# Norms of the first 400 tokens from squared columns, in an encoder layer on one core

## The chip, the core and the metric

The kernel runs on one core of one Trainium2 chip. The core has five engines with a queue of their own each: TensorE (PE; its weight loads are listed apart as PEld), VectorE (DVE), ScalarE (ACT), GpSimd (POOL) and SyncE (SP), which here issues nearly all transfers. A queue works strictly in its order; an instruction that waits holds up what stands behind it. The metric is the device time of one execution in microseconds (us), lower is better.

## What is computed

One layer of a hybrid encoder, run on a prompt of 256 tokens and a sample of 2048 tokens, each with 16 learned meta tokens ahead. Everything is float32.

```python
def rmsnorm(x, w):
    xf = x.astype(jnp.float32)
    y = xf * lax.rsqrt(jnp.mean(xf * xf, axis=-1, keepdims=True) + NORM_EPS)
    return (y * w.astype(jnp.float32)).astype(x.dtype)

def hybrid_layer(z, norm_w, w_in, q_norm_w, k_norm_w, sink, conv_w, conv_b, ln_w, ln_b, w_out):
    h = rmsnorm(z, norm_w)
    proj = jnp.einsum('bld,de->ble', h, w_in)
    q, k, v, g_att, c_val, c_glu, g_conv = jnp.split(proj, SPLIT_IDX, axis=-1)
...
    att = windowed_gqa(q, k, v, sink).reshape(B, L, W_ATT) * jax.nn.silu(g_att)
    cnv = conformer_conv(c_val, c_glu, conv_w, conv_b, ln_w, ln_b) * jax.nn.silu(g_conv)
    mixed = jnp.concatenate([att, cnv], axis=-1)
    return z + jnp.einsum('ble,ed->bld', mixed, w_out)
```

The change concerns the first line alone, `rmsnorm`, and of it the first 400 tokens (16 meta tokens and three blocks of 128).

## The kernel before

The tokens are kept as columns: `zt` is the transposed input, 1024 model dimensions as 8 slices of 128 partitions, and the 2320 columns are cut into six groups, the first of 400 columns (group 0), the others of 384. For each group a `Prep` object makes the normalised columns in two parts: `xh`, the value rounded to the form that TensorE multiplies in one pass, and `xl`, the rest. The weights of a unit of 256 output columns are split in the same way into `ws` high and low. One product of a group with half a unit is then 24 matmuls in one PSUM bank (8 slices by three passes: high by `xh`, high by `xl`, low by `xh`), and `pj` is the tile that it writes. The loop `items` runs over units and groups: the first two units take group 0, 1 and 2 in turn, so that the first four `pj` tiles, 96 matmuls, belong to group 0 and the next four to group 1. Then follow the other units, the convolution on DVE, attention and the output product.

How a group is prepared: `stats(i)` loads the rows of block i (`xn`, tokens on partitions; block 0 is the meta tokens), squares them on ACT with a running sum (`ssq`), and two POOL instructions (line 122 multiplies and adds, line 123 raises to the power -0.5) leave the factor in column i of `rstd`. `Prep.first` turns the factors of a group into a row `bc` in PSUM, the same on all partitions, by products with the identity. `Prep.scale(q)` multiplies two slices of `xt`, the loaded columns, by the norm weight and `bc` on DVE (line 681). `Prep.split(q)` rounds them on ACT into `xh` (line 698) and takes the differences `xl` (line 707), of each pair of slices the even one on DVE, the odd one on POOL. `weights(k)` loads a unit's weights as four pieces `wraw`, rounds each on ACT (line 742) and takes the low part on DVE or POOL (line 743).

What sets the order: a scheduler of the language places each engine's instructions by a time that it works out itself, except where a stretch is marked as `manual_schedule` for some engines or an instruction is pinned with `keep_in_program_order`; those keep the order in which the code is written. Transfers go out on SP in the order of its queue, over eight rotating semaphores, so that an issue waits until the transfer eight places earlier has landed. A tile is allocated from a pool with a fixed number of buffers, and a load into a buffer waits until its last reader is done: `xt` has four buffers, `us` (also used for `xn` of blocks 0 to 5 and for the second unit's `wraw`) four, `xn` of the later blocks two.

## Time and profile before

| | us |
|---|---|
| median of 3 runs (lowest, highest) | 976.84 (975.87, 977.05) |
| the profiled execution | 974.79 |
| its span, from the first to the last instruction | 973.0 |
| PE busy in the span | 949.2 |
| DVE, ACT, POOL busy | 755.9, 424.6, 341.2 |

The profile gives, for one execution, the start and length of every instruction, in us from the start of the span, and for an idle stretch the instruction or transfer that ended it. A row of the timeline merges equal instructions that follow each other: start, length from the first start to the last end, engine, line, operation, tile written and read, shape, count, and in brackets the idle time before it with what ended it. An ACT instruction that also sums its output shows as two rows. A float32 product with the identity is two matmuls in the profile.

### The profile page before, as it was taken

To read this page: it belongs to the slowest core of one execution; us is meant where nothing else is said; L and a number is where in the kernel's file an instruction comes from. 1 tells how busy PE (TensorE), PEld (TensorE's weight loads), DVE (VectorE), ACT (ScalarE), POOL (GpSimd) and SP (SyncE) were. 2 spreads that over 40 slices of the span, in tenths; PEclk is the share of its full clock that TensorE was granted. 3 is DMA by queue.
4 is the path that set the end of the run, shared out by engine and by line. 5 is a ranking of instruction groups with operands and counts; after the bars stand their busy time and mean duration, and the time that the engine had idled before them with its cause. 6 is when DMAs were issued, how large, how long until landed. Compare 5 with 4: busy or idle time off the path is not lost.

```text
span 973.0 us, 16234 instructions
## 1 busy us (share of the span) xinstructions
PE 949.2 (98%) x5740; PEld 890.0 (91%) x5740; DVE 755.9 (78%) x1261; ACT 424.6 (44%) x1156; POOL 341.2 (35%) x541
## 2 busy tenths in 40 slices
PE   5999999999999999999999998899999999999998
PEld 5999999999999999999999998678888888888886
DVE  4759999998987699999993555877776777767772
ACT  6621111343468710111113454766665666666651
POOL 5500000364468300000002464745445544544451
PEclk9999999999999999999999998999999999999999
DMA  9643345785735222233335657954554445544321
GB/s 332 221 181 118 130 170 179 264 286 182 225 124 180 92 73 76 86 128 136 127 135 173 212 141 219 294 171 134 159 177 148 125 152 166 178 127 135 109 88 43
DMA packets 113872, 155.75 MB, mean 160 GB/s; under 512 B 10592, under 2 KB 77296, under 8 KB 113792
## 3 DMA queue, kind: packets, MB, share of 16 engines
q1 hardware_dynamic: 113648, 154.11, 48.1%
q0 software_dynamic: 144, 0.62, 0.4%
q8 instruction: 45, 0.74, 0.3%
q14 instruction: 35, 0.29, 0.1%
HBM read 101.00 MB, written 54.31 MB: 160 GB/s over the span
## 4 chain that ended last, share of the span: by engine, by line
PE 91%; DMA 3%; DVE 2%; POOL 1%; issue 1%; SPq 1%; ACT 0%; POOLq 0%; DVEq 0%
PE pj L767 42%; PE y L538 20%; PE pj L783 13%; PE O L464 5%; PE pT L429 4%; PE S L316 4%; DMA woraw<-in_w_out 2%; DMA snk<-in_sink 1%; DMA wraw<-in_w_in 1%; PE O L316 1%; PE lnt L183 1%; PE qT L316 1%; PE lnu L202 1%; PE kt L941 0%; PE pT_m L426 0%
## 5 line engine op out<-in xcount | busy, mean ns | idle before, releaser
L767 PE MATMUL pj<-xh,ws 128*128 128x384 f32 (+1 forms) x1536 | 397.2, 339 | 2.5 <-ACT xh L698 2.5
L850 DVE SCALAR_TENSOR_TENSOR y<-us,cw,y 128x1167 f32<-128x1167 f32 x240 | 329.0, 1428 | 0.6
L767 PEld LDWEIGHTS pj<-xh,ws 128*128 128x128 f32 x1536 | 282.3, 189 | 2.8 <-ACT xh L698 2.8
L767 PE MATMUL pj<-xl,ws 128*128 128x384 f32 (+1 forms) x768 | 262.5, 342 | 0.1
L783 PE MATMUL pj<-ws,xh 128*128 128x256 f32 (+1 forms) x880 | 165.8, 286 | 0.0
L767 PEld LDWEIGHTS pj<-xl,ws 128*128 128x128 f32 x768 | 144.7, 188 | 1.1 <-POOL xl L707 0.7
L783 PEld LDWEIGHTS pj<-ws,xh 128*128 128x128 f32 (+1 forms) x880 | 137.8, 189 | 0.3
L783 PE MATMUL pj<-ws,xl 128*128 128x256 f32 (+1 forms) x440 | 125.4, 285 | 0.0
L383 ACT ACTIVATE sb<-sb,nm 128x304 f32<-128x304 f32 (+4 forms) x144 | 77.1, 535 | 45.3 <-DVE nm L371 43.7
L538 PE MATMUL y<-wo,mch 128*128 128x512 f32 x288 | 95.9, 414 | 0.0
L538 PE MATMUL y<-wo,mah 128*128 128x512 f32 x288 | 93.7, 406 | 0.0
L441 DVE TENSOR_TENSOR pl<-pT,ph 128x512 fp32r<-128x512 f32 x100 | 69.0, 690 | 29.0 <-ACT ph L440 28.5
L875 ACT ACTIVATE go<-pj 128x384 f32<-128x384 f32 x48 | 23.6, 491 | 154.5 <-PE pj L767 145.3
L371 DVE CUSTOM_DVE_ANT_0 sb<-S,bias,nsnk 128x304 f32<-128x304 f32 (+4 forms) x144 | 73.5, 511 | 15.0 <-PE S L316 14.5
L783 PEld LDWEIGHTS pj<-ws,xl 128*128 128x128 f32 (+1 forms) x440 | 83.2, 189 | 0.2
L122 POOL TENSOR_SCALAR ssk<-ssk 128x2 f32<-128x2 f32 x18 | 6.4, 356 | 213.0 <-ACT sqk L889 212.9
L440 ACT CAST ph<-pT 128x512 fp32r<-128x512 f32 x100 | 58.2, 583 | 40.2 <-PE pT L429 39.5
L406 POOL TENSOR_SCALAR sb<-sb,es 128x304 f32<-128x304 f32 (+4 forms) x144 | 72.8, 525 | 3.6
L316 PEld LDWEIGHTS S<-kw,q 128*128 128x128 f32 x288 | 53.8, 191 | 17.9 <-DVE nm L371 5.9
L122 POOL TENSOR_SCALAR ssq<-ssq 128x4 f32<-128x4 f32 (+2 forms) x55 | 28.3, 515 | 114.4 <-ACT xn L632 76.9
L316 PE MATMUL S<-kw,q 128*128 128x304 f32 (+4 forms) x288 | 62.6, 299 | 5.3 <-DVE nm L371 5.3
L429 PE MATMUL pT<-ident,sb 128*128 128x128 f32 x400 | 61.6, 274 | 1.3 <-POOL sb L406 1.0
(118 smaller groups left out, 1441.8 us busy)
## 6 DMA issues: line engine op xcount, KB each, us to landing
wd<-ws SPq DMA_DIRECT2D x36, 512.0 KB, 5.7
ws<-wd SPq DMA_DIRECT2D x36, 512.0 KB, 5.3
wraw<-in_w_in SPq DMA_DIRECT2D x52, 256.0 KB, 5.6
xn<-in_z SPq DMA_DIRECT2D x18, 512.0 KB, 5.7
gd<-go SPq DMA_DIRECT2D x48, 192.0 KB, 2.1
yo<-in_z SPq DMA_DIRECT2D x36, 256.0 KB, 2.6
out_y<-yo SPq DMA_DIRECT2D x36, 256.0 KB, 2.4
kw<-kd SPq DMA_DIRECT2D x16, 512.0 KB, 5.7
```

Of the source, the lines that this page charges most:

```text
L316: r = f(*a, **k)
L371: nc.vector.tensor_tensor_reduce(out=sb[:, n, c0:c1], in0=ps[:, 0:w], in1=cst["bias"][:, kv, n, c0 - QB * n : c1 - QB * n], scale=1.0, sca ...
L383: nc.scalar.activation(sb[:, n, c0:c1], sb[:, n, c0:c1], AF.Exp, bias=nm[:, n : n + 1], scale=-1.0, accum_out=rs[:, n : n + 1],)
L406: nc.gpsimd.tensor_scalar(sb[:, k, a0:a1], sb[:, k, a0:a1], es[:, k : k + 1], 1.0, op0=ALU.mult, op1=ALU.mult)
L429: nc.tensor.transpose(pt[:, hl, :], sbt[b, kv][:, hl, KCOL[k] : KCOL[k] + P], ident)
L440: nc.scalar.copy(ph, pt)
L441: nc.vector.tensor_tensor(pl, pt, ph, op=ALU.subtract)
L464: nc.tensor.matmul(o, lhs, t, start=(start and i == 0), stop=(stop and i == 1))
L538: nc.tensor.matmul(ps, mh[mi][:, e % 4, :], wo[e, wi][:, cols], start=(e == 4 and k == 0), stop=(e == 3 and k == 2),)
L767: nc.tensor.matmul(ps[:, :n], ws[:, d, wi, P * half_i : P * half_i + P], x[xi][:, d, o : o + n], start=(k == 0), stop=(k == 3 * ND - 1),)
L783: nc.tensor.matmul(ps[:rows, :UW], x[xi][:, d, o : o + rows], ws[:, d, wi, :], start=(k == 0), stop=(k == 3 * ND - 1),)
L850: nc.vector.scalar_tensor_tensor(y[:, yo + o0 : yo + o1], u[:, o0 + k : o1 + k], cw[:, j, k : k + 1], y[:, yo + o0 : yo + o1], op0=ALU.mul ...
```

## The change

The rows of blocks 0 to 3 are no longer loaded. The columns of group 0 are the first transfers. ACT squares each of the eight slices of 128x400 (`Prep.sums`), DVE adds them up in one tile, and four products with a column of ones (`ssq0`) sum over the partitions. DVE multiplies and adds, two POOL instructions raise to the power, and `first` goes on as before. TensorE multiplies the identity by itself into an unused tile `heat` 18 times ahead of these products, 8 times behind them and 6 times behind `first`. ACT, DVE and POOL keep the written order in this stretch (`MAN0`), and a few later instructions are pinned.

```diff
+MAN0 = {mybir.EngineType.Activation, mybir.EngineType.DVE, mybir.EngineType.Pool}
...
+    ones = const.tile([P, 1], F32, name="ones")
+    nc.vector.memset(ones, 1.0)
...
-                nc.scalar.activation(xn[:rows], xn[:rows], AF.Square, accum_out=ssq[:rows])
+                square = nc.scalar.activation(xn[:rows], xn[:rows], AF.Square, accum_out=ssq[:rows])
+                if i < 7:
+                    tc.keep_in_program_order(square)
...
+        def busy(pt, n):
+
+            for _ in range(n):
+                tc.keep_in_program_order(nc.tensor.matmul(pt[:, :P], ident, ident, start=True, stop=True))
...
+            def segments(self):
+                segs = [(0, NM, 0)] if self.g == 0 else []
+                return segs + [(blk_local(b)[1], P, b + 1) for b in range(3 * self.g, 3 * self.g + 3)]
+
+            def sums(self):
+
+                n = self.n
+                acc = None
+                for q in range(4):
+                    sq = cp.tile([P, UWID], F32, tag="us", name=f"sq{q}")[:, : 2 * 400].rearrange("p (d n) -> p d n", n=400)
+                    for dd in range(2):
+                        nc.scalar.activation(sq[:, dd, :n], self.xt[q][:, dd, :n], AF.Square)
+                        if acc is None:
+                            acc = sq[:, 0, :n]
+                        else:
+                            nc.vector.tensor_tensor(acc, acc, sq[:, dd, :n], op=ALU.add)
+                ps = psum.tile([P, 512], F32, tag="c", name="ssq0")
+                for o, rows, i in self.segments():
+                    tc.keep_in_program_order(
+                        nc.tensor.matmul(ps[:rows, i : i + 1], acc[:, o : o + rows], ones, start=True, stop=True)
+                    )
+                for rows, c0, c1 in ((P, 1, 4), (NM, 0, 1)):
+                    dst = rstd[:rows, c0:c1]
+                    nc.vector.tensor_scalar(dst, ps[:rows, c0:c1], 1.0 / D, EPS, op0=ALU.mult, op1=ALU.add)
+                    nc.gpsimd.tensor_tensor(dst, dst, half[:rows, 0 : c1 - c0], op=ALU.pow)
+
             def first(self):
...
-                    nc.tensor.matmul(
+                for o, rows, i in self.segments():
+                    pin(g == 1 and i == 4)(nc.tensor.matmul)(
...
-                nc.scalar.copy(hi, raw[q])
+                cast = nc.scalar.copy(hi, raw[q])
+                if k == 1:
+                    tc.keep_in_program_order(cast)
...
-        r = {i: stats(i) for i in (0, 1, 2, 3)}
+        for q in range(4):
+            preps[0].load(q)
         nc.sync.dma_start(vec, vecs)
-        preps[0].load(0)
-        preps[0].load(1)
         w01[0][0](nc.sync)
-        preps[0].load(2)
-        preps[0].load(3)
         nc.sync.dma_start(cw, conv_w)
         nc.vector.scalar_tensor_tensor(kscale, vec[:, 20:21], -(HD ** -0.5), vec[:, 21:22], op0=ALU.mult, op1=ALU.mult)
-        for i in (0, 1, 2, 3):
-            r[i]()
-        preps[0].first()
-        preps[0].alloc()
-        preps[0].scale(0)
-        for q in range(4):
-            if q < 3:
-                preps[0].scale(q + 1)
-            preps[0].split(q)
-            w01[0][1](q, nc.gpsimd if q % 2 else nc.vector)
+        heat = psum.tile([P, 512], F32, tag="d", name="heat")
+        with tc.manual_schedule(engines=MAN0):
+            busy(heat, 18)
+            preps[0].sums()
+            busy(heat, 8)
+            for q in range(4):
+                w01[0][1](q, nc.vector if q < 2 else nc.gpsimd)
+            preps[0].first()
+            busy(heat, 6)
+            preps[0].alloc()
+            preps[0].scale(0)
+            for q in range(4):
+                if q < 3:
+                    preps[0].scale(q + 1)
+                preps[0].split(q)
```

The change moves instructions beyond its own lines, since the scheduler lays out the rest anew. Three places matter below. The first is the start of DVE's queue from the last additions of the squares to the first difference `xl`; `sq_150` is the tile of the sum, `ws_0` the first unit's weights. Before:

```order
L998 SCALAR_TENSOR_TENSOR kscale<-vec 128x1
L681 SCALAR_TENSOR_TENSOR xt_0_116<-xt_0_116,vec,bc_151 128x400 x2
L681 SCALAR_TENSOR_TENSOR xt_1_118<-xt_1_118,vec,bc_151 128x400 x2
L743 TENSOR_TENSOR ws_0_120<-wraw_0_121,ws_0_120 128x2x256
L707 TENSOR_TENSOR xl_157<-xt_0_116,xh_156 128x400
```

Now:

```order
L1030 SCALAR_TENSOR_TENSOR kscale<-vec 128x1
L679 TENSOR_TENSOR sq_150<-sq_150,sq_159 128x400
L679 TENSOR_TENSOR sq_150<-sq_150,sq_164 128x400 x2
L687 TENSOR_SCALAR rstd<-ssq_169 128x3
L687 TENSOR_SCALAR rstd<-ssq_169 16x1
L778 TENSOR_TENSOR ws_0_118<-wraw_0_119,ws_0_118 128x2x256
L778 TENSOR_TENSOR ws_0_118<-wraw_1_121,ws_0_118 128x2x256
L714 SCALAR_TENSOR_TENSOR xt_0_109<-xt_0_109,vec,bc_194 128x400 x2
L714 SCALAR_TENSOR_TENSOR xt_1_111<-xt_1_111,vec,bc_194 128x400 x2
L740 TENSOR_TENSOR xl_206<-xt_0_109,xh_205 128x400
```

Additions, two small instructions and two weight differences now stand ahead of the first scaling, and the three last additions stand behind `kscale`, which needs the transfer `vec`.

The second place is PE's queue around the factors of group 1 (`bc_317` before, `bc_359` now); `pj_290` and `pj_353` before, `pj_332` and `pj_395` now, are the third and fourth tile of group 0. Before:

```order
L767 MATMUL pj_260<-xl_157,ws_0_120 128x400
L767 MATMUL pj_260<-xh_156,ws_0_120 128x400
L661 MATMUL bc_317<-ident,rstd 128x128 x2
L767 MATMUL pj_290<-xh_156,ws_1_196 128x400
L767 MATMUL pj_290<-xl_157,ws_1_196 128x400
L661 MATMUL bc_317<-ident,rstd 128x128
```

Now, at the end of the third tile and at the first matmuls of group 1:

```order
L802 MATMUL pj_332<-xh_205,ws_1_238 128x400 x2
L802 MATMUL pj_332<-xl_206,ws_1_238 128x400
L802 MATMUL pj_332<-xh_205,ws_1_238 128x400
L319 MATMUL bc_359<-ident,rstd 128x128 x3
L802 MATMUL pj_395<-xh_205,ws_1_238 128x400 x2
```

```order
L802 MATMUL pj_395<-xh_205,ws_1_238 128x400
L319 MATMUL bc_470<-ident,rstd 128x128 x3
L802 MATMUL pj_443<-xh_363,ws_0_118 128x384
L802 MATMUL pj_500<-xh_363,ws_0_118 128x384
L802 MATMUL pj_526<-xh_363,ws_1_238 128x384
L802 MATMUL pj_443<-xl_364,ws_0_118 128x384
```

The factors of group 1 came after 48 matmuls of group 0 and now come after 80 of its 96 (all 24 of `pj_332` and 8 of `pj_395` in between), those of group 2 (`bc_470`) now stand ahead of group 1's first matmul.

The third place is ACT's queue over the same stretch; `xn_389` to `xn_393` are the rows of blocks 7 to 9, which group 2 needs, `sg_1_0` is the sigmoid of `pj_332`. Before:

```order
L810 ACTIVATE sg_0_0_258<-pj_233 128x400
L698 CAST xh_321<-xt_0_213 128x384 x2
L698 CAST xh_321<-xt_1_217 128x384 x2
L698 CAST xh_321<-xt_2_221 128x384
L632 ACTIVATE xn_347,ssq_389<-xn_347 128x1024
```

Now:

```order
L845 ACTIVATE sg_0_0_300<-pj_275 128x400
L635 ACTIVATE xn_389,ssq_431<-xn_389 128x1024
L635 ACTIVATE xn_391,ssq_435<-xn_391 128x1024
L635 ACTIVATE xn_393,ssq_439<-xn_393 128x1024
L845 ACTIVATE sg_1_0_357<-pj_332 128x400
L731 CAST xh_363<-xt_0_255 128x384 x2
```

The squares of three blocks now stand ahead of the first rounding of group 1, which they stood behind or among.

More of the change, by code (lines that the diff above doesn't have):

```diff
@@ L656, in first @@
                 bc = psum.tile([P, 512], F32, tag="c", name=f"bc{g}")
-                segs = [(0, NM, 0)] if g == 0 else []
-                for b in range(3 * g, 3 * g + 3):
-                    segs.append((blk_local(b)[1], P, b + 1))
-                for o, rows, i in segs:
-                    nc.tensor.matmul(
+                for o, rows, i in self.segments():
+                    pin(g == 1 and i == 4)(nc.tensor.matmul)(
                         bc[:, o : o + rows],
```

## The prediction, made before the changed kernel ran

> **What bounds the kernel now.** I read the page first, then the chain of waits, then the timeline of the first 50 us.
>
> ```profile
> span 973.0 us, 16234 instructions
> PE 949.2 (98%) x5740; PEld 890.0 (91%) x5740; DVE 755.9 (78%) x1261; ACT 424.6 (44%) x1156; POOL 341.2 (35%) x541
> 16.46 8.36 PE pj L767 x40
> 24.82 0.44 PE bc L661 x4
> 25.85 12.23 PE pj L767 x68
> 39.28 20.75 PE pj L767 x118
> ```
>
> PE is busy for 949.2 of 973.0 us, and from 16.46 on the chain (start, length, what) stays on PE at least to 60 us. 68 matmuls of mostly 400 columns in 12.23 us are 0.18 each, 118 of 384 columns in 20.75 are 0.176, and a product with the identity is two matmuls of 0.11, 0.22 together. So only the time by which PE gets through groups 0 and 1 counts; what it gains or loses there goes to the end undiminished. Its start:
>
> ```profile
> 13.00 1.04 PE L767 MATMUL pj<-xh,ws 128*128 128x400 f32 x2 [2.46 <-ACT xh L698]
> 24.66 0.61 PE L661 MATMUL bc<-ident,rstd 128*128 128x128 f32 x4
> 10.57 2.25 DVE L681 SCALAR_TENSOR_TENSOR xt<-xt,vec,bc 128x400 f32<-128x400 f32 x4 [2.54 <-PE bc L661]
> 11.90 0.62 ACT L742 CAST ws<-wraw 128x512 fp32r<-128x512 f32 x1 [3.12 <-DMA wraw<-in_w_in]
> 13.00:18.20 5.20, 5.07 (x13) 4.04 (x14) 1.00 1.05 400
> 18.20:24.66 6.46, 6.46 (x36) 6.28 (x35) 1.00 1.05 379
> ```
>
> The first `pj` matmul starts at 13.00: scaling began at 10.57, but ACT waited until 11.90 for the weights. The first 48 matmuls (two tiles) are through at 24.66, where `bc` of group 1 begins; of these, 13 start in the first 5.2 us and the rest at 0.18 each (windows: length, PE busy, weight loads, granted clock). So 24.66 is the mark that the change has to beat.
>
> **The change part by part: the factors.** Four transfers of `xt` (400 KB each) take the place of 64 KB and three times 512 KB, the same 1600 KB.
>
> ```profile
> 7.63 1.06 ACT L632 ACTIVATE xn<-xn 128x1024 f32<-128x1024 f32 x1 [0.18 <-DMA xn<-in_z]
> 7.87 0.16 DVE L998 SCALAR_TENSOR_TENSOR kscale<-vec 128x1 f32<-128x1 f32 x1 [7.00 <-DMA vec<-in_vecs]
> 13.37 0.94 ACT L698 CAST xh<-xt 128x400 fp32r<-128x400 f32 x2
> 13.35 0.57 DVE L707 TENSOR_TENSOR xl<-xt,xh 128x400 fp32r<-128x400 f32 x1
> 9.14 0.54 POOL L123 TENSOR_TENSOR rstd<-ssq,half 128x1 f32<-128x1 f32 x1
> 12.75 0.69 DVE L743 TENSOR_TENSOR ws<-wraw,ws 128x512 fp32r<-128x512 f32 x1
> ```
>
> The last bytes are in at 7.6, `vec` lets `kscale` end at 8.0. The last two squares cost what two roundings of this shape cost, 0.94, and end at 8.6. But three additions stand behind `kscale`, each needs the one before, and each costs what a difference of this shape does, 0.57, with 0.07 between: 8.0 + 3 x 0.64 = 9.9. Four products with the column of ones are eight matmuls that load full weights, at 0.11: 10.8. DVE's small instruction is put at `kscale`'s 0.16: 11.1. Then two powers of 0.54 one behind the other: 12.2. So much if nothing disturbs POOL. But DVE's next rows are two weight differences of 0.69, and POOL and DVE get in each other's way:
>
> ```profile
> 13.54 1.52 POOL L743 TENSOR_TENSOR ws<-wraw,ws 128x512 fp32r<-128x512 f32 x1 [3.86 <-ACT ws L742]
> 14.35 1.14 DVE L707 TENSOR_TENSOR xl<-xt,xh 128x400 fp32r<-128x400 f32 x1 [0.44 <-ACT xh L698]
> 32.48 2.33 DVE L707 TENSOR_TENSOR xl<-xt,xh 128x384 fp32r<-128x384 f32 x3
> 34.48 0.74 POOL L123 TENSOR_TENSOR rstd<-ssq,half 128x1 f32<-128x1 f32 x1
> 29.02 2.08 POOL L707 TENSOR_TENSOR xl<-xt,xh 128x384 fp32r<-128x384 f32 x2 [1.28 <-ACT xh L698]
> ```
>
> A difference on DVE of 0.57 that starts at 14.35, while POOL works until 15.06, ends at 15.49: 0.43 behind POOL. A power at 34.48, beside the last of three DVE differences (to 34.81), takes 0.74, not 0.54. Taking turns, power, difference, power, difference, the second power ends at 13.3. The products of `first` begin with the meta block, whose factor is that second power. They take 4 x 0.22, so scaling starts at about 14.4 (13.3 without collisions: the 8 identity products, 1.8 from 10.8, end at 12.6, then 0.9 less what overlaps). Before, it started at 10.57.
>
> The Trainium skill, page "SBUF — State Buffer", section "Who interferes with whom", says that a DVE instruction with two SBUF inputs and a GpSimd instruction that reads SBUF exclude each other for the whole instruction, whoever comes first. By it the collisions are certain and the start is 14.4, not 13.3; the 1.14 above agrees.
>
> **From scaling to PE at work.** The weights no longer decide, having come earlier. DVE does four scalings (2.25) before the first `xl`. ACT rounds slice 1 by 1.7 after the start of scaling (0.62, 0.94, waits of 0.07), and POOL then takes its difference, 1.04 (half of 2.08). DVE's first `xl` comes 0.43 behind it: 1.7 + 1.04 + 0.43 = 3.2 (2.8 if DVE is first). Until then PE has but two matmuls to do, behind 6 identity products (1.3). So it resumes at 14.4 + 3.2 = 17.6 and does the other 46 in 46 x 0.18 = 8.3: 25.9 against 24.66, **1.2 later** (-0.1 with 13.3 and 2.8; the end above is the clock's, below).
>
> **Group 1.** The second edit is not in the diff: `bc` of group 1 now stands behind 80 matmuls, not 48.
>
> ```profile
> 39.32 4.29 DVE L681 SCALAR_TENSOR_TENSOR xt<-xt,vec,bc 128x384 f32<-128x384 f32 x8 [3.87 <-PE bc L661]
> 43.52 2.88 DVE L707 TENSOR_TENSOR xl<-xt,xh 128x384 fp32r<-128x384 f32 x3
> 32.06 0.42 SPq L626 DMA_DIRECT2D xn<-in_z  x1
> 36.56 1.06 ACT L632 ACTIVATE xn<-xn 128x1024 f32<-128x1024 f32 x1 [2.33 <-POOL xl L707]
> ```
>
> Behind it DVE needs eight scalings, 4.2, and its first `xl`, 1.1 behind POOL (the first 1.1 of the 2.88): 5.3. PE has 16 matmuls (2.9), three products of `bc` for group 2 (0.7) and three matmuls with `xh` (0.5): 4.1. It then waits 1.2. ACT is no earlier: its squares of blocks 7 to 9 now stand ahead of the sigmoid and of the first `xh`, and block 9's row is loaded into a buffer that block 7's square has to free. From that issue to the next square went 4.5 in the row at 32.06, with one more transfer ahead; that puts the first roundings about where DVE ends its scalings and POOL's differences a turn later. I take **1.5** (0.5 if the turns fall well, 2.5 if block 9 takes the full 4.5). Before, this cover was 48 matmuls, and no wait of PE is listed there. The number of all other products is the same; from group 2 on there is a tile's time to spare on each side.
>
> **The clock.** The 32 identity products lie beside the wait for factors and are hidden, save in the 12.6 above. Their use depends on this:
>
> ```profile
> 1.01 0.29 POOL masks.py:199 TENSOR_SCALAR_AFFINE_SELECT ident<-ident 128x128 f32<-128x128 f32 x1
> 599.44 0.73 PE L316 MATMUL S<-kw,q 128*128 128x176 f32 x2 [3.42 <-DVE nm L371]
> 595.10:598.50 3.40, 0.92 (x9) 0.71 (x6) 0.20 (x1) 0.84 (x2) 0.00 (x0) 1.00 0.91 283
> 598.50:605.30 6.80, 5.86 (x27) 5.86 (x28) 5.98 (x19) 5.10 (x15) 4.29 (x7) 0.50 0.74 240
> 622.40:625.80 3.40, 1.78 (x6) 0.78 (x6) 3.30 (x7) 2.74 (x9) 2.76 (x6) 1.00 1.07 374
> 623.34 1.57 PE L429 MATMUL pT<-ident,sb 128*128 128x128 f32 x4 [1.04 <-POOL sb L406]
> 625.80:629.20 3.40, 3.07 (x11) 2.69 (x11) 3.36 (x7) 1.86 (x5) 2.22 (x3) 0.50 1.09 352
> ```
>
> The granted clock falls to 0.50 for 3.4 or 6.8 us after 3.4 us in which PE was busy 0.92, or 1.78. In the new start PE can multiply the identity from 1.4 on. If the slow pace lasts as long as the 5.2 us at 13.00, it does twelve of the 18 at 0.44 and six at 0.22, done at 7.9. It is idle to 9.9, 2.0 us, and again from about 16 to 17.6. Either gap can leave an interval of 3.4 us half idle, and 3.4 us at half pace cost 1.7: in full behind 17.6, and 1.0 ahead of it, where 0.7 (12.6 to 13.3) lie beside the powers. Nothing is lost if both gaps fall across two intervals. I take **0.8**, between none and the 2.7 of both, since 1.78 busy was too little.
>
> The Trainium skill, page "TensorE: Matmul & The Clock Gate", section "Why this matters for your kernels", warns only of gaps above about 3 us. By it these gaps cost nothing and the sum is 2.7. The rows disagree: the longest wait in the interval from 622.40 was 1.04, and the clock fell.
>
> **Sum.** 1.2 + 1.5 + 0.8 = 3.5 later. The profiled execution took 974.79 (span 973.0, 1.8 around it), so 978.3 of its kind; the median of the runs, 976.84, is 2.05 above it, so 980.3 of theirs.
>
> **Rivals.** *Faster: a warm PE with early factors.* The half-pace stretch from 13.0 to 18.2 costs before (5.2 - 13 x 0.18 = 2.9), and the change removes it if scaling starts early enough. Were `vec` in 0.5 sooner, the products with ones one pass (0.5), the powers undisturbed and `first` at 0.11 each, scaling would start at 11.6; 2.8 later is 14.4, plus 8.3 gives 22.7, 2.0 sooner, and with no wait at group 1 the time is 974.8. For it: ACT's wait for weights is gone. Against: `kscale` and the power rows. It decides from a start of scaling at 11.7 down. *No change: turns fall well.* Scaling at 13.3, `xl` 2.8 behind, clock kept: -0.1, and 1.0 at group 1, 977.7. For it: POOL's first `xl` and DVE's start only 0.5 apart. Against: two powers and two differences are bound to meet. *The clock isn't held at all.* The identity products are then work for nothing: four, eight and four products at twice 0.22 add 3.5 less the 0.7 beside the powers, and a slow pace of 5.2 us behind 17.6 adds 2.6; with the 2.7 that is 8.1, 984.9. For it the row at 622.40; against it, PE works six us without a break at first. *The loss is absorbed later* at the waits near 600 us: no row before 590 us shows PE idle, so these start as much later; 976.8, hardly.
>
> **How the numbers follow.** A change counts as faster or slower beyond 0.2%, 2.0 us, about what a measurement of this kernel can tell. Forecast, 2 to 6.4 later (1.2 + 2.5 + 2.7 at most): 0.65. Clock not held at all: 0.05. No change by well-placed turns 0.17, by absorption 0.03. Faster, 0.1. So slower 0.7, same 0.2, faster 0.1. The range reaches from 976.0, just below the well-placed turns with no wait at group 1, to 983.2, the forecast with the clock lost twice; left out are the faster case and the clock never held, under 2 in 10. The forecast's own range is 978.8 to 983.2.
>
> **What would show it.** The first scaling (line 714) at 14.4, behind powers (line 688) that take over 0.6 or start over 0.6 apart; the second `pj` pair's last matmul near 26; a wait of PE for DVE's `xl` of 1 to 2 us near 37, and `bc` of group 2 ahead of it; for the clock, products at half pace for some 3 us between 10 and 21, or none. A start of scaling before 12, or group 1 without a wait, would make the prediction wrong.

## The result, and the profile after

The changed kernel took 980.37 us (median of 8 runs, 978.31 to 982.49), the kernel before 976.85 beside it (8 runs, 975.87 to 978.76): a ratio of 1.0035 with a 95% interval of 1.0022 to 1.0047, 3.5 us slower. The forecast was 980.3. The profiled execution took 979.06, that of the kernel before 974.79, which is 2.1 below its median; so the ends of two single executions are not compared below.

The head of the page of the changed kernel, then TensorE's timeline (start, length, instruction, count, idle time ahead of it and what ended that):

```profile
span 977.3 us, 16381 instructions
PE 957.2 (98%) x5812; PEld 899.5 (92%) x5812; DVE 756.0 (77%) x1271; ACT 423.5 (43%) x1156; POOL 337.6 (35%) x535
```

```profile
1.35 6.80 PE L647 MATMUL heat<-ident 128*128 128x128 f32 x36 [1.35 <-POOL ident masks.py:199]
10.05 0.96 PE L683 MATMUL ssq<-ones,sq 128*16 128x1 f32 x8 [1.90 <-DVE sq L679]
10.87 2.03 PE L647 MATMUL heat<-ident 128*128 128x128 f32 x16
13.78 1.25 PE L319 MATMUL bc<-ident,rstd 16*128 16x16 f32 x8 [0.87 <-POOL rstd L688]
14.87 1.50 PE L647 MATMUL heat<-ident 128*128 128x128 f32 x12
...
18.40 0.45 PE L802 MATMUL pj<-xl,ws 128*128 128x400 f32 x1 [1.45 <-DVE xl L740]
...
32.73 0.83 PE L319 MATMUL bc<-ident,rstd 128*128 128x128 f32 x6
36.31 0.83 PE L319 MATMUL bc<-ident,rstd 128*128 128x128 f32 x6
...
38.68 0.44 PE L802 MATMUL pj<-xl,ws 128*128 128x384 f32 x1 [1.01 <-DVE xl L740]
```

PE is 8 us busier than before and the kernel is slower: most of what was added is identity products, which advance nothing. Steady work starts at 18.40, behind a wait for the first `xl`, and the next wait is the one at 38.68, behind the products of `bc` for group 2, at the place the prediction named. DVE and POOL ahead of that second wait:

```profile
33.59 4.29 DVE L714 SCALAR_TENSOR_TENSOR xt<-xt,vec,bc 128x384 f32<-128x384 f32 x8 [4.25 <-PE bc L319]
37.80 2.10 DVE L740 TENSOR_TENSOR xl<-xt,xh 128x384 fp32r<-128x384 f32 x2
...
36.23 4.55 POOL L740 TENSOR_TENSOR xl<-xt,xh 128x384 fp32r<-128x384 f32 x4 [0.39 <-ACT xh L731]
```

The late `bc` lets DVE start its eight scalings at 33.59. Its first `xl` follows them without a pause at 37.80, finds POOL's second difference running (37.20 to 38.21) and ends at 38.62, 0.41 behind it; undisturbed it would take 0.55.

What the start waits for is on DVE:

```profile
7.33 0.57 DVE L679 TENSOR_TENSOR sq<-sq,sq 128x400 f32<-128x400 f32 x1 [0.29 <-ACT sq L675]
7.98 0.16 DVE L1030 SCALAR_TENSOR_TENSOR kscale<-vec 128x1 f32<-128x1 f32 x1
8.06 1.93 DVE L679 TENSOR_TENSOR sq<-sq,sq 128x400 f32<-128x400 f32 x3
11.05 0.21 DVE L687 TENSOR_SCALAR rstd<-ssq 128x3 f32<-128x3 f32 x2 [1.06 <-PE ssq L683]
11.19 1.27 DVE L778 TENSOR_TENSOR ws<-wraw,ws 128x512 fp32r<-128x512 f32 x2
15.07 2.25 DVE L714 SCALAR_TENSOR_TENSOR xt<-xt,vec,bc 128x400 f32<-128x400 f32 x4 [2.60 <-PE bc L319]
17.24 1.10 DVE L740 TENSOR_TENSOR xl<-xt,xh 128x400 fp32r<-128x400 f32 x1
```

The additions end at 9.99, scaling starts at 15.07, and the first `xl` is done at 18.34, 3.27 later. Between 11.05 and 15.07 lie the two powers, here with their shapes kept apart (busy time, mean ns of one):

```profile
L688 POOL TENSOR_TENSOR rstd<-rstd,half 128x3 f32<-128x3 f32 x1 | 1.9, 1906 | 10.0 <-DVE rstd L687 10.0
L688 POOL TENSOR_TENSOR rstd<-rstd,half 16x1 f32<-16x1 f32 x1 | 0.5, 547 | 0.0
```

The power beside DVE's two weight differences takes 1.91, the one behind them 0.55.

All later sections use one measure beside the time: when the 48th and the 144th `pj` product start (the 48th of group 0 and the 48th of group 1), read from each trace. The column on half clock ahead of 30 us says until when TensorE ran at half clock from the start on, or for how long it lost full clock again once it had it; times in us.

| kernel | first scaling | 48th product | 144th product | half clock ahead of 30 us | half clock, 595 to 640 us | profiled execution | median (runs) | before beside it |
|---|---|---|---|---|---|---|---|---|
| before | 10.57 | 24.48 | 42.97 | to 18.2 | 10.2 | 974.79 | 976.85 (8) | |
| changed | 15.07 | 26.71 | 46.49 | none from 6.7 on | 13.7 | 979.06 | 980.37 (8) | 976.85 |
| 1: no identity products | 16.55 | 29.67 | 48.17 | to 23.2 | 13.7 | 981.21 | 981.40 (5) | 977.17 |
| 2: one power | 16.48 | 28.11 | 47.79 | 6.8 | 13.7 | 980.47 | 978.80 (10) | 977.17 |
| 3: group 1 early | 14.88 | 26.51 | 45.01 | none | 10.2 | 977.13 | 978.79 (12) | 977.17 |
| 4: before, with identity products | 10.53 | 25.18 | 43.65 | none | 17.1 | 979.48 | 978.55 (11) | 977.17 |
| 5: power undisturbed | 14.56 | 29.80 | 49.82 | 10.2 | 10.2 | 980.27 | 982.52 (6) | 977.18 |
| 6: `xh` products first | 15.34 | 26.27 | 46.49 | none | 10.2 | 977.72 | 979.07 (10) | 977.18 |
| 7: four edits | 15.26 | 26.19 | 44.72 | 6.8 | 17.1 | 978.93 | 978.03 (11) | 977.18 |
| 8: root and reciprocal | 15.01 | 25.17 | 43.64 | 3.4 | 10.2 | 977.92 | 977.92 (11) | 977.18 |
| 9: gap filled | 16.98 | 28.63 | 48.48 | 3.4 | 10.2 | 980.72 | 980.22 (7) | 977.28 |
| 10: four edits, warm | 14.17 | 25.11 | 43.64 | none | 13.7 | 978.43 | 977.37 (12) | 977.28 |
| 11: root, warm | 13.09 | 23.56 | 42.03 | none | 10.2 | 976.33 | 976.09 (12) | 977.28 |
| 12: rows, warm | 10.12 | 22.68 | 41.43 | none | 10.2 | 975.71 | 976.86 (12) | 977.48 |

The changed kernel stands 26.71 - 24.48 = 2.23 later at the 48th product, and 46.49 - 42.97 = 3.52 later at the 144th: 1.29 more at group 1. The medians differ by 3.52 as well. A single execution doesn't settle 1 or 2 us: every trace loses clock where attention begins, for 10.2 to 17.1 us in all, and 3.4 us at half clock are up to 1.7. So the mechanism is read from the table's first columns, the size from the medians. What is lost early stays lost for long: at the 2500th product the changed kernel is 3.93 behind (434.89 against 430.96). The changed kernel was timed in one series, so a difference between it and an experiment is uncertain by about 1.5 us (two standard errors, from the spread of the runs).

### The profile page after: what moved, and what is told of

It is laid out like the page before. It is cut to its first block, busy times and chain, and to the rows that moved or that the text cites. A ratio compares the mean times of both kernels' runs of the same rounds, so it can differ in the third digit from the quotient of the medians.

```text
span 977.3 us, 16381 instructions
## 1 busy us (share of the span) xinstructions
PE 957.2 (98%) x5812; PEld 899.5 (92%) x5812; DVE 756.0 (77%) x1271; ACT 423.5 (43%) x1156; POOL 337.6 (35%) x535
## 4 chain that ended last, share of the span: by engine, by line
PE 88%; DVE 3%; DMA 3%; POOL 2%; issue 1%; SPq 1%; ACT 1%; POOLq 0%; DVEq 0%; ACTq 0%
PE pj L802 41%; PE y L541 19%; PE pj L818 12%; PE O L467 4%; PE pT L432 4%; PE S L319 4%; DMA woraw<-in_w_out 2%; PE O L319 1%; PE qT L319 1%; DMA wraw<-in_w_in 1%; PE lnt L186 1%; DVE xt L714 1%; PE lnu L205 1%; DMA msk<-in_mmask 0%; POOL xl L740 0%
## 5 line engine op out<-in xcount | busy, mean ns | idle before, releaser
L374 DVE CUSTOM_DVE_ANT_0 sb<-S,bias,nsnk 128x304 f32<-128x304 f32 (+4 forms) x144 | 73.4, 511 | 14.4 <-PE S L319 13.8
L125 POOL TENSOR_SCALAR ssq<-ssq 128x4 f32<-128x4 f32 (+1 forms) x51 | 25.0, 491 | 113.4 <-ACT xn L635 74.1
```

Source lines behind the costliest of these rows:

```text
L374: nc.vector.tensor_tensor_reduce(out=sb[:, n, c0:c1], in0=ps[:, 0:w], in1=cst["bias"][:, kv, n, c0 - QB * n : c1 - QB * n], scale=1.0, sca ...
```

## The experiments

**1. Without the identity products.**

```diff
-            busy(heat, 18)
             preps[0].sums()
-            busy(heat, 8)
...
-            busy(heat, 6)
```

> The changed kernel without its 32 identity products; nothing else is edited, but the order made for TensorE then puts bc of group 1 behind 72 products instead of 80. My account (the products keep the clock up): a half-pace stretch of about 5 us appears behind the first real products at 16 to 18 us and costs 2.6, and the earlier bc takes up to 1.25 off the wait near 38, so 980.4 + 2.6 - 1.25 = 981.8, and the granted clock is 0.5 between about 16 and 23 us. Rival (TensorE would have been granted full clock anyway, or loses it anyway): no half-pace stretch beyond the changed kernel's, only the earlier bc counts, 979.1 to 980.4. The start of scaling (15.1) stays where it is by both, since the powers (to 13.7) set it.

Measured: 981.40, a ratio of 1.0050 (1.0038 to 1.0062), near the 981.8 of my account and above the rival's range, though the interval overlaps that of the changed kernel. TensorE's timeline:

```profile
14.33 2.18 PE L319 MATMUL bc<-ident,rstd 16*128 16x16 f32 x8 [2.77 <-POOL rstd L688]
...
20.38 0.87 PE L802 MATMUL pj<-xh,ws 128*128 128x400 f32 x2
...
23.28 0.53 PE L802 MATMUL pj<-xh,ws 128*128 128x400 f32 x2
```

A pair of products takes 0.87 until 23.2 and 0.53 from there. The 48th product comes 2.96 later than in the changed kernel: half of that before scaling (which I had expected to stay; `bc` takes 2.18 instead of 1.25 and the products with ones 1.58 instead of 0.96), half behind it. At the 144th only 1.68 is left, since `bc` of group 1 stood at 72 products here and its wait is gone. So the identity products are worth 3.0 us at the start, where I had expected 2.6, and half of it lies at a place where I had expected nothing.

**2. One power in place of two, and 3 identity products behind the sums instead of 8.**

```diff
-                        nc.tensor.matmul(ps[:rows, i : i + 1], acc[:, o : o + rows], ones, start=True, stop=True)
+                        nc.tensor.matmul(ps[:, i : i + 1], acc[:, o : o + P], ones, start=True, stop=True)
...
-                for rows, c0, c1 in ((P, 1, 4), (NM, 0, 1)):
+                for rows, c0, c1 in ((P, 0, 4),):
...
-            busy(heat, 8)
+            busy(heat, 3)
```

> The changed kernel with one power of 128x4 in place of two (the ones-product of the meta block takes 128 columns, so that all rows of its column are written; the factors used are the same), and 3 identity products instead of 8 behind the ones-products, so that these (to 12.9 before) don't take the powers' place as the last in. My account (the two powers of 2.43 together are two turns with the two weight differences): one power ends at 11.9 with no turn or 12.5 with one, bc starts behind it, scaling at 13.2 to 13.9 instead of 15.1, and all of the 1.2 to 1.9 goes to the end: 978.5 to 979.2. Rival (powers of this shape take 1.2 by themselves, and no turns are taken): the one power takes 1.2 or more, scaling at 13.9, 979.2. Second rival (time before group 1 is taken up by the wait for group 1, which hangs on transfers): scaling earlier, but the wait near 38 grows by as much, 980.4.

Measured: 978.80, 1.0021 (1.0012 to 1.0030); 1.6 above the kernel before where the changed kernel is 3.5 above, so 1.9 was won in the median, the upper end of what I expected. The trace doesn't show this gain. The profiled execution, the slowest of the ten, has a poor start: its sums ended 1.4 later (11.4 against 9.99), behind transfers that came late. GpSimd's and VectorE's timelines, then the stretches ahead of and behind the loss of clock (length, busy time of PE, PEld, DVE, ACT and POOL, granted clock, DMA):

```profile
12.80 1.41 POOL L688 TENSOR_TENSOR rstd<-rstd,half 128x4 f32<-128x4 f32 x1 [11.50 <-DVE rstd L687]
...
12.63 1.30 DVE L778 TENSOR_TENSOR ws<-wraw,ws 128x512 fp32r<-128x512 f32 x2
```

```profile
9.33:12.74 3.41, 1.28 (x11) 1.28 (x12) 1.99 (x6) 3.16 (x6) 0.00 (x0) 1.00 1.05 411
12.74:16.15 3.41, 2.83 (x13) 2.50 (x13) 1.19 (x2) 0.00 (x0) 3.35 (x3) 0.50 1.03 382
```

The one power ends at 14.21, 0.28 behind the second difference (13.93). And the clock is at 0.50 for 6.8 us, so that scaling starts 3.93 behind DVE's small instruction (12.55), no sooner than in the changed kernel (4.02).

**5. The power alone on its port.** The two weight differences of DVE stand behind the first four scalings; the rest is as in number 2. `los` collects the four differences of the first unit, so that they can be issued later.

```diff
-            busy(heat, 8)
+            busy(heat, 3)
+            los = []
             for q in range(4):
-                w01[0][1](q, nc.vector if q < 2 else nc.gpsimd)
+                w01[0][1](q, nc.gpsimd, los)
+            los[2]()
+            los[3]()
...
+                if q == 0:
+                    los[0]()
+                    los[1]()
                 preps[0].split(q)
```

> As the kernel with one power and 3 identity products behind the ones-products, but VectorE's two weight differences stand behind the first four scalings instead of beside the power. My account (the power is long because it waits for a turn behind the differences): the power takes 0.55 to 0.6 instead of 1.41, and scaling starts 0.8 sooner after the sums than with the differences beside it; but the two differences, 1.3 and more beside GpSimd's own two, now lie between scaling and the first xl, so TensorE resumes no sooner: 979.3 to 981. Rival (a power of 128x4 is that long by itself): 1.4 again, no sooner start, and 980.5 to 982.

Measured: 982.52, 1.0051 (1.0039 to 1.0063), later than either expected.

```profile
11.26 1.03 POOL L688 TENSOR_TENSOR rstd<-rstd,half 128x4 f32<-128x4 f32 x1 [9.96 <-DVE rstd L687]
...
16.73 2.66 DVE L779 TENSOR_TENSOR ws<-wraw,ws 128x512 fp32r<-128x512 f32 x2
...
16.37 2.47 POOL L740 TENSOR_TENSOR xl<-xt,xh 128x400 fp32r<-128x400 f32 x2 [1.62 <-ACT xh L731]
```

With nothing on DVE beside it the power takes 1.03, not the 0.55 to 0.6 that I expected and not the rival's 1.4. So a power of four columns is twice as long as one of one column, and the differences add 0.4 to it. The differences themselves now take 2.66 instead of 1.27, beside POOL's first two `xl`: the collision moved to the path and grew. This execution also lost full clock for 10.2 us, so how much of the late 48th product (29.80) comes from the collision is not told apart.

**3. Group 1's factors early.**

```diff
-                    pin(g == 1 and i == 4)(nc.tensor.matmul)(
+                    nc.tensor.matmul(
...
                 r[5]()
+                r[6]()
                 for q in range(4):
                     preps[1].load(q)
                     w01[1][1](q, nc.gpsimd if q % 2 else nc.vector)
-                r[6]()
```

> The changed kernel with the square of block 6 ahead of the second weights' roundings on ScalarE and bc of group 1 no longer pinned: bc of group 1 then stands behind 48, 48 and 52 products (as before: 48, 48, 50) and the roundings of group 1 ahead of the square of block 9. My account: the 1.25 wait near 38 us goes, 979.1, and the start to 26.9 us is unchanged. Rival (bc early only moves the collisions: DVE scales while it should take the second weights' differences, and TensorE waits for these near 27): a new wait of 0.5 to 1.5 near 27 to 30, 979.6 to 980.6.

Measured: 978.79, 1.0018 (1.0008 to 1.0028): 1.6 above the kernel before instead of 3.5. The trace lists no wait of TensorE near 38; from the 48th product to the 144th it takes 45.01 - 26.51 = 18.50, as before (18.49), where the changed kernel takes 19.78. The whole 1.29 is the order at group 1. ScalarE's timeline shows the second half of the edit, roundings ahead of the last square:

```profile
31.59 2.16 ACT L731 CAST xh<-xt 128x384 fp32r<-128x384 f32 x5
34.02 1.06 ACT L635 ACTIVATE xn<-xn 128x1024 f32<-128x1024 f32 x1 [0.27 <-DMA xn<-in_z]
```

**6. `xh` products first.**

```diff
-            for d in range(ND):
-                for wi, xi in PASSES:
...
+            order = [(d, wi, xi) for d in range(ND) for wi, xi in PASSES]
+            if pj_n[0] <= 2:
+                order.sort(key=lambda s: s[0] + 3 * (s[1] + s[2] > 0))
+            for d, wi, xi in order:
...
```

> The changed kernel with TensorE's order alone changed in the first two tiles: the products that need only xh run three slices ahead of those with xl and with the low weights, so 6 instead of 2 products stand ahead of the first xl. My account (from scaling on, TensorE waits for the first xl only, and group 1 is bound by TensorE reaching its bc): the wait of 1.45 at 16.9 shrinks to 0.4 to 0.7, the 48th product starts at 25.6 to 25.9 instead of 26.7, the wait near 38 stays 1.2 to 1.4, and 0.8 to 1.1 go to the end: 979.4. Rival (group 1 is bound by the transfer and square of block 9, which don't come sooner): the wait near 38 grows by the same, 980.4.

Measured: 979.07, 1.0023 (1.0013 to 1.0032). The interval holds the 979.4 of my account and ends just below the rival's 980.4, but it overlaps that of the changed kernel, so the time settles little. The profile speaks for the rival. The wait ahead of the first `xl` shrinks to 0.39 and the 48th product comes 0.44 sooner, but ScalarE, VectorE and TensorE at group 1 read:

```profile
33.80 1.06 ACT L635 ACTIVATE xn<-xn 128x1024 f32<-128x1024 f32 x1 [1.27 <-DMA xn<-in_z]
...
35.24 3.40 ACT L731 CAST xh<-xt 128x384 fp32r<-128x384 f32 x8
...
33.31 4.29 DVE L714 SCALAR_TENSOR_TENSOR xt<-xt,vec,bc 128x384 f32<-128x384 f32 x8 [3.67 <-PE bc L319]
37.52 2.41 DVE L740 TENSOR_TENSOR xl<-xt,xh 128x384 fp32r<-128x384 f32 x2
...
38.69 0.45 PE L804 MATMUL pj<-xl,ws 128*128 128x384 f32 x1 [1.47 <-DVE xl L740]
```

The square of block 9 starts at 33.80 and the roundings at 35.24 here and in the changed kernel alike, the wait grows from 1.01 to 1.47, and the 144th product starts at 46.49 in both. DVE scales 0.28 sooner here and reaches its first `xl` at 37.52, not 37.80, but that `xl` ends at 38.63 against 38.62: it finds POOL's second difference running, which ends at 38.22 and 38.21 and goes back to the roundings at 35.24, behind block 9's square. So a `bc` that comes only 0.28 sooner wins nothing. Block 9's row alone would not win much either: in the changed kernel DVE is busy with its scalings up to the `xl`, which could end at 38.35 at the earliest (37.80 + 0.55), 0.27 sooner. The wait hangs on both, the late `bc` with eight scalings and then a turn behind POOL.

**4. The kernel before with identity products.**

```diff
+        heat = psum.tile([P, 512], F32, tag="d", name="heat")
+        with tc.manual_schedule(engines=MAN0):
+            for i in (0, 1, 2, 3):
+                r[i]()
+            busy(heat, 24)
+            p0.first()
+            busy(heat, 6)
...
```

> The kernel before, with the instructions of VectorE, ScalarE and GpSimd of its start in its own order, plus 24 identity products ahead of the first bc and 6 behind it; no column squares. Group 1's bc stands behind 48, 48 and 52 products (before: 48, 48, 50). My account: TensorE has full clock from 13.0 on, so the 2.9 that half pace costs from 13.0 to 18.2 is no longer the limit; the feeding by xl becomes it, and from the durations of the rows the 48th product comes about 1.2 sooner than at 24.66, 975.7 in the end (974.0 if feeding never limits). Rival (half pace is hidden behind feeding in full, or the pauses at 13 to 17 us lose the clock again): 976.8 or later, with 0.5 in the clock between 13 and 20 us.

Measured: 978.55, 1.0017 (1.0008 to 1.0026), the rival's time, but not for a lost clock: TensorE has full clock from 6.3 on, and the 48th product still comes 0.7 later than before. TensorE, VectorE and GpSimd:

```profile
15.00 0.45 PE L790 MATMUL pj<-xl,ws 128*128 128x400 f32 x1 [1.69 <-DVE xl L722]
...
13.30 3.00 DVE L722 TENSOR_TENSOR xl<-xt,xh 128x400 fp32r<-128x400 f32 x2
...
13.23 1.29 POOL L730 TENSOR_TENSOR ws<-wraw,ws 128x512 fp32r<-128x512 f32 x1 [3.46 <-ACT ws L726]
```

DVE's first `xl` comes 0.07 behind the start of POOL's weight difference and has to let it finish; before, it started 0.19 ahead of it and took 0.57. The two `xl` take 3.00, and the third product, the first to use one, starts at 15.00 instead of 13.97. The weights had reached ACT 0.3 sooner, and with them POOL's difference came 0.3 sooner, DVE's `xl` 0.05. A warm TensorE that is fed no sooner just waits.

**7 and 8. All edits at once, in two ways.** Number 7 puts together one power, 3 identity products, `kscale` behind the sums, number 3 and number 6. Number 8 takes the factors from ACT's square root and DVE's reciprocal.

```diff
-        nc.vector.scalar_tensor_tensor(kscale, vec[:, 20:21], -(HD ** -0.5), vec[:, 21:22], op0=ALU.mult, op1=ALU.mult)
...
             preps[0].sums()
+            nc.vector.scalar_tensor_tensor(kscale, vec[:, 20:21], -(HD ** -0.5), vec[:, 21:22], op0=ALU.mult, op1=ALU.mult)
...
+            def factors(self):
+                dst = rstd[:, 0:4]
+                nc.scalar.activation(dst, self.ssq[:, 0:4], AF.Sqrt, bias=eps, scale=1.0 / D)
+                nc.vector.reciprocal(dst, dst)
```

> The changed kernel with one power, 3 identity products behind the ones-products, kscale behind the sums, block 6's square ahead of the second weights with bc of group 1 unpinned, and the xh products three slices ahead. My account (the losses add up as I split them): 1.2 to 1.9 for the power, 0.3 for kscale, 1.3 for group 1, 0.8 to 1.1 for the xh products, together 3.6 to 4.6 off 980.4: 975.8 to 976.8, level with the kernel before or just ahead of it. Rival (they overlap: what comes sooner at the start waits for the second weights or for the transfers at 23 to 27): 977.5 to 978.5.

> The changed kernel with the factors from a square root on ScalarE and a reciprocal on VectorE instead of powers on GpSimd, kscale behind them, one weight difference of VectorE ahead and one behind, each slice split as soon as it is scaled, and group 1's squares ahead of three of the four second weights with its bc pinned behind 48, 52 and 64 products. The values are the same to rounding. My account (the powers, the turns and the group 1 order are the whole loss): scaling starts at 12.3 to 12.8, the 48th product at 23.2 to 23.8 (26.7 in the changed kernel, 24.5 before), no wait near 38, 975.2 to 976.3 in the end, faster than the kernel before by 0.5 to 1.5. Rival (VectorE and GpSimd take turns over the differences, so feeding and not the factors sets the pace): the 48th product at 24.5 or later, 977 or more.

Measured: 978.03, 1.0010 (1.0001 to 1.0018), and 977.92, 1.0003 (0.9995 to 1.0012), 1.2 and 1.6 above my ranges. These are the rivals' times, but not for their reasons. Of number 7, VectorE's additions, then the clock:

```profile
6.72 3.29 DVE L679 TENSOR_TENSOR sq<-sq,sq 128x400 f32<-128x400 f32 x5
```

```profile
7.48:10.89 3.41, 1.87 (x18) 1.68 (x16) 2.22 (x4) 1.98 (x5) 0.00 (x0) 1.00 0.94 310
10.89:14.30 3.41, 3.09 (x14) 2.76 (x14) 1.43 (x4) 1.54 (x3) 2.78 (x3) 0.50 1.03 411
```

Without `kscale` in front the additions end at 10.01, as in the changed kernel (9.99): five of them follow each other without a pause, and `kscale` held up next to nothing. And full clock is lost for 6.8 us, as in number 2; both have 3 identity products behind the sums instead of 8. In number 8 it was lost for 3.4, with transfers that came 1 us later (`bc` again takes over 2):

```profile
7.72 2.00 ACT L677 ACTIVATE sq<-xt 128x400 f32<-128x400 f32 x4 [1.54 <-DMA xt<-in_zt]
...
12.79 2.19 PE L321 MATMUL bc<-ident,rstd 16*128 16x16 f32 x8
```

**9. The changed kernel with 25 identity products ahead of the sums.**

```diff
-            busy(heat, 18)
+            busy(heat, 25)
```

> The changed kernel with 25 identity products ahead of the sums instead of 18, so that TensorE works from 1.4 to about 9.9 without the pause of 1.9 us; nothing else of the start is edited. My account (the pause costs the clock in some executions, though not in the profiled one of the changed kernel, as it did in three executions with fewer products behind it): full clock until 16 us in the profile, scaling at 15.1 as before, and the median comes down by a part of the 2.6 that a lost stretch cost: 979.2 to 980.2, with fewer executions above 981. Rival (with 8 products behind the sums the clock is never lost, or the added products hold up the sums): 980.4 or later, and the same spread.

Measured: 980.22, 1.0027 (1.0016 to 1.0037), against 1.0035 (1.0022 to 1.0047) without the edit: no difference that can be told. (None of its 7 runs is above 981, two of the changed kernel's 8 are.) Its profiled execution had late transfers, a pause of 2.33 all the same, and lost the clock:

```profile
8.44:11.86 3.42, 1.09 (x11) 0.88 (x10) 2.38 (x5) 3.20 (x8) 0.00 (x0) 1.00 1.06 404
11.86:15.27 3.41, 3.41 (x18) 3.41 (x18) 1.41 (x4) 0.55 (x1) 2.53 (x3) 0.50 0.99 384
```

So the trace doesn't show what a filled pause is worth.

**10 and 11. Numbers 7 and 8 with more identity products** (here number 10; in number 11 the 23, and 6 instead of 5 behind `bc`).

```diff
-            busy(heat, 18)
+            busy(heat, 23)
...
-            busy(heat, 3)
+            busy(heat, 7)
```

> The kernel of the four edits with 23 identity products ahead of the sums instead of 18 and 7 instead of 3 behind them. My account (cutting the products from 8 to 3 lost the clock at 10.9 us and with it what the shorter power gained): full clock from about 7 us on, the power ends at 12.9, scaling at 14.1 instead of 15.3, the 48th product at 25.0 instead of 26.2, and 976.6 to 977.2 in the end. Rival (the clock is lost in the wait for scaling anyway, or the seven products hold bc up): 978.0 again.

> The kernel with root and reciprocal, with 23 identity products ahead of the sums instead of 18 and 6 instead of 5 behind bc. My account: full clock from about 7 us on, bc done in 1.25 instead of 2.19, scaling at 12.9 to 13.8, the 48th product at 23.3 to 24.0, 976.0 to 976.7, faster than the kernel before by 0.5 to 1.2. Rival (the xt transfers, which came 1 us later in that execution, set the start, and the clock is lost in the wait for the factors as before): 977.5 to 978.

Measured: 977.37, 0.9997 (0.9988 to 1.0007), and 976.09, 0.9992 (0.9982 to 1.0002). Both keep full clock in the start. Of number 10, TensorE and GpSimd, then of number 11 TensorE:

```profile
12.88 1.25 PE L694 MATMUL bc<-ident,rstd 16*128 16x16 f32 x8
...
11.36 1.47 POOL L688 TENSOR_TENSOR rstd<-rstd,half 128x4 f32<-128x4 f32 x1 [10.05 <-DVE kscale L1036]
```

```profile
11.80 1.25 PE L321 MATMUL bc<-ident,rstd 16*128 16x16 f32 x8 [0.18 <-DVE kscale L1067]
...
15.24 0.45 PE L830 MATMUL pj<-xl,ws 128*128 128x400 f32 x1 [0.28 <-DVE xl L760]
```

In number 10 scaling starts at 14.17 and the 48th product at 25.11, as expected within about 0.1; the median is 0.7 lower than that of number 7 and 0.2 above my range. Number 11 starts scaling at 13.09 and comes to the 48th product at 23.56, 3.15 sooner than the changed kernel and 0.92 sooner than the kernel before. In time it is level with the kernel before: 1.2 us ahead in the median, with an interval that just holds 1, so the gain I expected is not shown.

**12. Rows instead of columns, in a good order.** The kernel before, with identity products as in number 4 and the start in an order that gives DVE the first `xl` early.

```diff
+            p0.scale(0)
+            p0.scale(1)
+            p0.xh1(0, 0)
+            w_hi(0)
+            p0.xh1(0, 1)
+            p0.xl1(0, 0, nc.vector)
+            w_lo(0, nc.vector)
...
```

> The kernel before (factors from rows, no column squares) with 24 identity products ahead of the first bc and 6 behind it, its first differences and roundings in another order (first two slices scaled, first xh ahead of the first weights, first xl ahead of the first weight difference), and the group 1 order of the kernel with root and reciprocal. My account (a warm TensorE and an order without bad turns are what can be won, and the column squares win nothing by themselves): scaling at 10.5 against 13.1 there, but the weights of the first slices come later (roundings from 11.6), feeding sets the pace, and the 48th product starts at 23.0 to 23.8, as there (23.6): 975.3 to 976.3, level with it. Rival (the later weights and the turns of GpSimd and VectorE eat it as in the kernel before with identity products, 48th at 25.2): 977.3 or more, and then the column squares are worth 1 us or more with the right order.

Measured: 976.86, 0.9993 (0.9984 to 1.0002).

```profile
12.91 0.63 PE L800 MATMUL pj<-xl,ws 128*128 128x400 f32 x2 [0.40 <-DVE xl L730]
```

The first `xl` is used at 12.91 instead of 15.00 in number 4, and the 48th product starts at 22.68, 0.3 sooner than I expected; the time is 0.6 later than the range. Numbers 11 and 12 can't be told apart by it. So no gain of the column squares themselves is seen.

## Why the prediction was right

The time was right (980.37 against 980.3), the direction and both places too. That it came so close is luck: the start cost 2.23 instead of 1.2, group 1 1.29 instead of 1.5, and the clock nothing in the profiled execution instead of 0.8, and these errors cancel.

- *The factors.* Additions to 9.99 (forecast 9.9), products with ones and DVE's small instructions to 11.26 (11.1): right. For the two powers I had 2.2 with collisions, from 11.1 to 13.3. They took 2.43, to 13.72. The collision is there, but the step that failed is the price of a power, 0.54 alone and 0.74 beside a difference, whatever its width: number 5 shows 1.03 for four columns with nothing beside it. Between 0.55 and 1.03, three columns would take some 0.87 alone (an estimate), so that about 1.0 of the 1.91 is collision. Then `bc` took 1.25 where I had 0.88. Scaling started at 15.07 instead of 14.4, and the terms I gave add up to 14.2 only.
- *`kscale`.* The additions ended where I said, but not because they stood behind it. With and without it (number 7) they end at 9.99 and 10.01: behind the squares of the third slice, four or five additions that wait for each other are the limit.
- *From scaling to `xl`.* 3.27 against 3.2, and by the steps named: POOL's first difference ends at 17.91, DVE's `xl` 0.43 behind it. Then 8.3 from 18.40 to the start of the 48th product, 0.2 more than forecast. Of the 1.0 by which the start cost more than forecast, 0.7 lies ahead of the first scaling.
- *Group 1.* 1.29 against 1.5, of which the one wait is 1.01. Number 3 takes it away whole. My account gave two limits, DVE behind a late `bc` and ACT behind block 9's row; the rows at 33.59 and 36.23 show the first as the longer one, and the second as a turn of 0.27 at its end. Number 3 eases both at once, and how much of the 1.29 an early `bc` alone would win stays open.
- *The clock.* Forecast 0.8, none in the profiled execution. The interval of the result, 2.1 to 4.6 us, doesn't tell whether other executions lost some, and number 9, meant to fill the first pause, left one of 2.33 in its trace. So what this term is worth in the median stays open. It isn't idle: numbers 2, 5, 7, 8 and 9 lost 3.4 to 10.2 us of full clock at or soon behind this place in their profiled executions.
- *The rivals.* The faster case asked for a start of scaling by 11.7. Number 11 reached 13.09 and was level with the kernel before. That half pace costs the kernel before 2.9 was half the truth: number 4 took it away and won nothing, since the first `xl` set the pace, and with an early `xl` number 12 won 1.8 at the 48th product (22.68 against 24.48), which the time doesn't show clear of noise. In the case of well-placed turns, 13.3, 2.8 and 8.3 give 0.3 sooner than 24.66, not 0.1; it changes no conclusion.

The Trainium skill, page "SBUF — State Buffer", section "Who interferes with whom", calls the port that VectorE and GpSimd share an exclusive lock. Number 4 agrees for two differences (0.07 us decided over 1.0). A power and a difference disturb each other, 1.41 against 1.03 alone, but number 2 shows no lock for the whole of both: the power ended 0.28 behind the second difference, having run beside the two, and these took 0.69 each, as one does undisturbed in number 8. Scalings, which read `bc` from PSUM, don't show it: four took 2.25 beside POOL's differences in the changed kernel and 2.25 before.

## What to carry to other kernels

A shorter way to a small result has to be counted to its last step: here the row loads and running sums went, and a chain of additions, a product, a power beside two differences and another product took their place on the path, 4.5 us later in all. Before a start is put in another order, list which VectorE and GpSimd differences will now meet, since a shift of 0.3 us turned who goes first in number 4 and cost 1.0. Identity products have to be counted again after every edit of the path: numbers 2, 5 and 7, with 18 ahead of the sums and 3 behind, lost full clock, numbers 10 and 11, with 23 ahead, kept it. These are single executions, and number 9 lost it with 25 and 8, so the count alone does not decide.

## What the runs showed of the hardware

- *The clock falls after shorter pauses than expected, and no single share of busy time decides.* In number 7 it fell behind a stretch of 3.41 us with PE busy for 1.87 and one listed wait of 1.54; in the changed kernel it stayed up behind a stretch as long with 1.51 and a wait of 1.90:

```profile
6.66:10.07 3.41, 1.51 (x14) 1.32 (x14) 2.75 (x6) 2.23 (x5) 0.00 (x0) 1.00 0.93 262
```

  The Trainium skill, page "TensorE: Matmul & The Clock Gate", section "Why this matters for your kernels", warns of pauses above about 3 us; number 7 disagrees. Where in time the hardware draws its stretches, these records don't show.
- *A power on GpSimd grows with its columns:* 0.55 for one, 1.03 for four.
- *A difference on VectorE that finds one of GpSimd running ends 0.4 behind it:* 0.43 in the kernel before (15.06 to 15.49) and in number 4 (14.52 to 14.95), 0.43 and 0.41 in the changed kernel (17.91 to 18.34, 38.21 to 38.62). Alone it takes 0.55 to 0.57.
- *The same transfers in the same order land over 1 us apart.* The squares of the third slice started at 6.61 (number 7), 6.75 (changed kernel) and 7.95 (number 9), and with them everything up to the 48th product. These are executions of three programs with the same first transfers. One execution of each program was profiled, so it is not shown that starts differ as much between executions of one program; the runs of the changed kernel spread over 4.2 us.
